# Modulation loads on GpSimd's queue, the last head's output kept on chip, and the first gate multiplied into the output weights

## The chip, the cores and the metric

The kernel runs on one core of a Trainium2 chip. The core has TensorE (PE, matrix products), VectorE (DVE), ScalarE (ACT), GpSimd (POOL) and SyncE (SP, which here only starts transfers), each of which works through its own instructions in order, and 16 DMA engines. The metric is the device time of one execution in microseconds (us), the median of several runs.

## The reference

One layer of a transformer block on x of 1024 positions by 1024 features, with six vectors of modulation from a conditioning vector c. Cut to what matters:

```python
mod = silu(c) @ w_ada + b_ada
sh_m, sc_m, gt_m, sh_f, sc_f, gt_f = split(mod, 6)

h = rms_norm(x, g_mix) * (1 + sc_m) + sh_m
qa, ka, va, qb, kb, vb = split(h @ w_in)
o_a = neighbourhood_attention(qa, ka, va, rpb)         # 8 heads of 64
o_b = differential_attention(qb, kb, vb, lam, slopes)  # 4 heads, two maps each
o_b = rms_norm(o_b, subln_w) * (1 - lambda_init)       # per head
mix = concat(o_a, o_b) @ w_out
x = x + gt_m * mix

h = rms_norm(x, g_ffn) * (1 + sc_f) + sh_f
gate, up = split(h @ w_gate_up)
x = x + gt_f * ((silu(gate) * up) @ w_down)
out = rms_norm(x, g_final)
```

All is float32. The gate gt_m scales columns of mix, so it may as well scale the columns of w_out.

## The kernel before

Each product of two float32 matrices is made of three passes on PE: both factors are split into a high part and a rest (names ending in h and l), and high by high, rest by high and high by rest are summed in PSUM. For every operand ACT makes the high part and DVE or POOL subtracts it (line 202 for weights, a raw tile of 128x1024 with the suffix r from one of two buffers). Matrix products are mostly 128x512.

The stages follow each other. **Start-up**: x is loaded, normalised (`rs` on POOL, a scaling on DVE) and turned; the first two modulation vectors are summed up on DVE. **Attention**: 64 units in a row, `Na` for four pairs of neighbourhood heads of eight units each, then `Da` for four differential heads of eight units. A unit has a score, a softmax on DVE and ACT, a turn of the weights on PE (`nt` or `at`) and a product with v (`npv` or `pv`). The loop over units calls the score of the next unit, `pv` of the last, norm and finish of those before, and between these `fill`, which takes products of the input projection (`q`, `k`, `v`) for later heads out of a queue. When these are done (last unit of the third `Da` head), `load_late` reads back the first four blocks of the attention's output from DRAM (`ol`), splits them and loads half of the output weights (`wo`); then `gen_mo` makes the first half of the output projection (blocks n = 0 to 3, tiles `mo`) as filler of the last head, multiplies each tile by the gate (`mt`) and adds it to x.

**The drain**: the last unit's `pv`, its norm (`ms`, `rda`, `bc`), and its store to DRAM. Then pool `mx` closes, `lp` takes its memory, and blocks 4 to 7 are loaded and split into it with the other half of the weights. The second half of the projection (tiles `mp`, n = 4 to 7) runs, each tile is multiplied by the gate (`mu`, line 1053) and added (line 1054, on POOL up to i = 5). **norm2** and the **feed-forward** stage (`gu` gate and up, `dn` down) follow.

**Modulation**: vectors 2 to 5 are summed by `gen_mods` (lines 570 to 607), a generator taken one step per unit: each half vector has eight steps, a load `wm` of 256 KB and a multiply-add into `acc` on DVE. Vectors 2, 3 and 4 (48 loads) run during attention; 2 is `gate_m`. Vector 5, `gate_f`, runs beside the first feed-forward group. All these loads are issued by SP. The bias tables of a pair, `tz`, are loaded by SP in `tables` when the pair starts.

The order in the program: in the start-up and for the first two units, PE, DVE, ACT and SP keep the order in which the code is written, while POOL does not; behind that a scheduler places instructions on every engine by their dependences and by its own estimate of when they are ready. Pools with a number of buffers (bufs) make a writer wait until the reader of the buffer's last tile is done.

Of the kernel before, what the change touches and what calls it, by code (L numbers as in the profile page):

```python
# [19 lines left out]
P = 128  # L20
# [84 lines left out]
def block_kernel(ctx: ExitStack, tc: tile.TileContext, t: dict):  # L105
# [449 lines left out]

    def tables(pr):
        tb = []
        for m in range(2):
            h = 2 * pr + m
            tbh = np_.tile([P, 896], F32, tag="tb", bufs=2, name=f"tb{h}")  # L560
            tz = mp.tile([P, 384], F32, tag="sq", bufs=4, name=f"tz{h}")
            z = t["rpb"]
            SY.dma_start(out=tz, in_=bass.AP(tensor=z.tensor, offset=z.offset + 512 * h + 1, ap=[[1, P], [1, 384]]))
# [7 lines left out]
    def gen_mods(steps, raw_of, acc_of, tmp_of, gate, ahead=2):  # L571
# [76 lines left out]
    class Da:  # L648
# [90 lines left out]
        def finish(self):  # L739
# [114 lines left out]
    def gate_m():  # L854
        if 2 not in gates:
# [4 lines left out]
                    lambda nm, dt=F32: mp.tile([P, 512], dt, tag="sq", bufs=4, name=nm), gate_m)  # L860
# [3 lines left out]
    def load_o(n, pool, **kw):  # L864

        if n % 4 == 0:
            for z, lst in (("h", oh), ("l", ol)):
                lst.append([pool.tile([P, 4, 512], F32R, name=f"o{z}{n}{b}", **kw) for b in range(2)])
        for b in range(2):
            SY.dma_start(out=ol[n // 4][b][:, n % 4, :].bitcast(F32), in_=o_dram[n][:, b * 512:(b + 1) * 512])  # L870

    def split_o(n):
        for b in range(2):
            dh, dl = oh[n // 4][b][:, n % 4, :], ol[n // 4][b][:, n % 4, :]
            A.activation(out=dh, in_=dl.bitcast(F32), func=AF.Copy)
            V.tensor_tensor(out=dl, in0=dl.bitcast(F32), in1=dh.bitcast(F32), op=ALU.subtract)

    def load_wo(dh, n2, split):
        raw = raw_t(f"wo{dh}_{n2}r")
        SY.dma_start(out=raw, in_=t["w_out"][dh, n2])  # L880
        wo[dh].append(split(raw, f"wo{dh}_{n2}"))

    def load_late():
        lo_eng[:] = [V]
        for n in range(4):
# [302 lines left out]
```

## Time and profile before

| what | us |
|---|---|
| median of three runs | 1437.06 (1435.95 to 1438.21) |
| the profiled execution | 1438.62 |
| its span, first to last instruction | 1436.9 |
| PE busy | 1375.6 |
| DVE, ACT, POOL busy | 736.2, 462.7, 275.6 |

The mean granted clock of PE was 0.974 of full speed. Busy time counts no waits, no DMA issues and no semaphores; PE's matrix products overlap, so a full-speed product of 128x512 shows some 390 ns of its own though the next begins about 227 ns after it. A row of a timeline names the instruction by its line, its engine and its tiles (out<-in), and in brackets the idle time before it and what ended that. All products have line 89, a helper's. The window from 8 to 60 us is the start-up, attention lasts until about 641 us, the drain until about 708 and the feed-forward stage to the end.

### The profile page before, as it was taken

How to read it: one execution, taken by the hardware profiler on the slowest of the kernel's cores; microseconds unless marked ns; L12 is line 12 of the kernel's file. 1: busy time of each engine (PE TensorE's matmuls, PEld its weight loads, DVE VectorE, ACT ScalarE, POOL GpSimd, SP SyncE). 2: the span in 40 equal slices, each digit the busy share in tenths (PEclk: the TensorE clock that was granted, in tenths of full speed). 3: DMA queues.
4: the chain of work that ended last, by engine and by line, in shares of the span. 5: the costliest groups of instructions: out<-in, count | busy, mean ns of one | idle time of the engine just before them, and what ended most of it. 6: DMA issues, size and time to landing. Idle time of an engine off the chain costs nothing.

```text
span 1436.9 us, 17706 instructions
## 1 busy us (share of the span) xinstructions
PE 1375.6 (96%) x7033; PEld 1137.9 (79%) x7033; DVE 736.2 (51%) x1336; ACT 462.7 (32%) x817; POOL 275.6 (19%) x274
## 2 busy tenths in 40 slices
PE   5899998899999999988999999999999999999997
PEld 5698777787897777766878888888888888888886
DVE  5775866758777587767737315212411431152136
ACT  5544444444544464423440210211021111202212
POOL 3021221210002100003430420422132122204201
PEclk8999998999999999998999999999999999999999
DMA  9231522423021251006111210211021111102102
GB/s 380 91 118 48 182 99 83 151 95 111 23 89 59 96 198 38 8 29 221 59 44 59 88 31 29 82 36 59 15 73 59 30 59 59 44 16 88 44 15 103
DMA packets 47826, 115.34 MB, mean 80 GB/s; under 512 B 12755, under 2 KB 14035, under 8 KB 46464
## 3 DMA queue, kind: packets, MB, share of 16 engines
q1 hardware_dynamic: 47632, 114.05, 23.4%
q8 instruction: 55, 0.90, 0.3%
q14 instruction: 27, 0.22, 0.0%
q0 software_dynamic: 112, 0.17, 0.0%
HBM read 99.52 MB, written 14.68 MB: 79 GB/s over the span
## 4 chain that ended last, share of the span: by engine, by line
PE 86%; DMA 6%; DVE 5%; issue 1%; ACT 1%; SPq 0%; POOL 0%; DVEq 0%; POOLq 0%; ACTq 0%
PE gu L89 33%; PE dn L89 17%; PE s L89 4%; PE mo L89 3%; PE q L89 3%; PE pv L89 3%; PE k L89 3%; PE mp L89 2%; PE nk L89 2%; DMA wm<-in_w_ada_l_dram 2%; PE at L89 2%; PE v1p L89 2%; PE npv L89 2%; PE v2p L89 2%; DMA w_r<-in_w_in_dram 2%; PE sps L89 2%
## 5 line engine op out<-in xcount | busy, mean ns | idle before, releaser
L1095 DVE TENSOR_TENSOR sg<-sg,gu 128x512 f32<-128x512 f32 x44 | 30.2, 687 | 354.5 <-ACT sg L1094 354.3
L89 PE MATMUL dn<-wd_l,ah 128*128 128x512 f32 x352 | 137.0, 389 | 0.0
L89 PE MATMUL dn<-wd_h,al 128*128 128x512 f32 x352 | 137.0, 389 | 0.0
L89 PE MATMUL dn<-wd_h,ah 128*128 128x512 f32 x352 | 137.0, 389 | 0.0
L1125 DVE TENSOR_TENSOR dt<-dn,gate_f 128x512 f32<-128x512 f32 x96 | 66.3, 691 | 87.7 <-PE dn L89 87.7
L202 POOL TENSOR_TENSOR wg_l<-wg_r,wg_h 128x1024 fp32r<-128x1024 f32 x20 | 47.9, 2396 | 295.6 <-ACT wg_h L201 295.6
L201 ACT ACTIVATE wg_h<-wg_r 128x1024 fp32r<-128x1024 f32 x22 | 23.3, 1061 | 225.3 <-PE dn L89 165.7
L675 ACT ACTIVATE p<-p,st 128x1024 f32<-128x1024 f32 x64 | 73.4, 1148 | 68.3 <-DVE st L673 68.0
L673 DVE CUSTOM_DVE_ANT_0 p<-s,dist 128x1024 f32<-128x1024 f32 x64 | 76.6, 1218 | 16.2 <-PE s L89 16.0
L89 PE MATMUL s<-qk 64*128 64x512 f32 x384 | 80.4, 427 | 2.2 <-DVE st L673 2.1
L202 POOL TENSOR_TENSOR wd_l<-wd_r,wd_h 128x1024 fp32r<-128x1024 f32 x20 | 47.9, 2397 | 161.1 <-ACT wd_h L201 161.1
L89 PEld LDWEIGHTS dn<-wd_l,ah 128*128 128x128 f32 x352 | 66.1, 188 | 13.7
L89 PEld LDWEIGHTS dn<-wd_h,al 128*128 128x128 f32 x352 | 66.1, 188 | 13.7
L89 PEld LDWEIGHTS dn<-wd_h,ah 128*128 128x128 f32 x352 | 66.1, 188 | 13.7
L1126 DVE TENSOR_TENSOR x<-x,dt 128x512 f32<-128x512 f32 x96 | 70.0, 729 | 2.9
L89 PE MATMUL gu<-h2h,wg_h 128*128 128x512 f32 x176 | 68.6, 390 | 1.9 <-DVE sg L1095 1.9
L202 POOL TENSOR_TENSOR w_l<-w_r,w_h 128x1024 fp32r<-128x1024 f32 x19 | 47.3, 2497 | 119.7 <-ACT w_h L201 113.1
L1094 ACT ACTIVATE sg<-gu 128x512 f32<-128x512 f32 x44 | 25.9, 589 | 137.1 <-PE gu L89 133.3
L89 PE MATMUL gu<-h2l,wg_h 128*128 128x512 f32 x176 | 68.5, 389 | 0.0
L89 PE MATMUL gu<-h2h,wg_l 128*128 128x512 f32 x176 | 68.5, 389 | 0.0
L89 PE MATMUL gu<-h2l,wu_h 128*128 128x512 f32 x176 | 68.5, 389 | 0.0
L89 PE MATMUL gu<-h2h,wu_l 128*128 128x512 f32 x176 | 68.5, 389 | 0.0
(287 smaller groups left out, 3483.7 us busy)
## 6 DMA issues: line engine op xcount, KB each, us to landing
wm<-in_w_ada_l_dram SPq DMA_DIRECT2D x64, 256.0 KB, 3.7
w_r<-in_w_in_dram SPq DMA_DIRECT2D x24, 512.0 KB, 4.2
wg_r<-in_w_gate_up_dram SPq DMA_DIRECT2D x22, 512.0 KB, 3.6
wu_r<-in_w_gate_up_dram SPq DMA_DIRECT2D x22, 512.0 KB, 3.5
wd_r<-in_w_down_dram SPq DMA_DIRECT2D x22, 512.0 KB, 3.5
x<-in_x_dram SPq DMA_DIRECT2D x16, 512.0 KB, 8.8
wada<-in_w_ada_s_dram SPq DMA_DIRECT2D x6, 1024.0 KB, 12.1
v<-vd SPq DMA_DIRECT2D x4, 1024.0 KB, 4.9
```

Of the source, the lines that this page charges most:

```text
L89: ins = call(*args, **kw)
L201: A.activation(out=hi, in_=raw, func=AF.Copy)
L202: lo_engine().tensor_tensor(out=lo, in0=raw, in1=hi.bitcast(F32), op=ALU.subtract)
L673: V.tensor_tensor_reduce(out=pr, in0=s, in1=dists[0][:, d0:d0 + 1024], scale=1.0, scalar=BIG, op0=ALU.add, op1=ALU.min, accum_out=self.st[ ...
L675: A.activation(out=pr, in_=pr, func=AF.Exp, scale=-1.0, bias=self.st[:, m:m + 1], accum_out=self.st[:, 2 + m:3 + m])
L1094: A.activation(out=sg, in_=gu[:, 0:512], func=AF.Silu)
L1095: V.tensor_tensor(out=sg, in0=sg, in1=gu[:, 512:1024], op=ALU.mult)
L1125: V.tensor_tensor(out=dt_, in0=out, in1=gtf[:, dsl], op=ALU.mult)
L1126: V.tensor_tensor(out=x1[i][:, dsl], in0=x1[i][:, dsl], in1=dt_, op=ALU.add)
```

## The change

It has three parts. The loads `wm` of vectors 2 to 4 are issued by GpSimd instead of SyncE, and so are the table loads `tz`, which are now started at the seventh unit of the pair before (for the first pair at the beginning); vector 5's loads stay with SyncE, and its first accumulation is placed behind the last add of the output projection. The first gate is multiplied into the raw output weights before they are split, eight multiplies of 128x1024 on DVE, and `mt` and `mu` are gone: tiles are added to x straight from PSUM, by DVE alone. And the last half head's output goes into a raw buffer (`o_last`) and is split from there, with no store and no reload; blocks 4 and 5 and the weights `wo0_2` and `wo1_2` are loaded at the last unit but one into a buffer of the attention's pool, four products' worth of tiles (`mpb0`, `mpb1`) are begun before the norm, and only blocks 6 and 7 and `wo0_3`, `wo1_3` are loaded behind it.

```diff
+    def load_tables(pr):
+        for m in range(2):
+            h = 2 * pr + m
+            tzs[h] = mp.tile([P, 384], F32, tag="sq", bufs=4, name=f"tz{h}")
+            z = t["rpb"]
+            G.dma_start(out=tzs[h], in_=bass.AP(tensor=z.tensor, offset=z.offset + 512 * h + 1, ap=[[1, P], [1, 384]]))
...
-    def gen_mods(steps, raw_of, acc_of, tmp_of, gate, ahead=2):
+    def gen_mods(steps, raw_of, acc_of, tmp_of, gate, queue, first=None, ahead=2):
...
-                SY.dma_start(out=raws[-1], in_=t["w_ada_l"][which - 2, n, :, j, :])
+                queue.dma_start(out=raws[-1], in_=t["w_ada_l"][which - 2, n, :, j, :])
...
-                V.tensor_scalar(out=acc, in0=raws[at], scalar1=silc[:, 0:1], scalar2=None, op0=ALU.mult)
+                head = V.tensor_scalar(out=acc, in0=raws[at], scalar1=silc[:, 0:1], scalar2=None, op0=ALU.mult)
+                if first is not None:
+                    PE.after(head, first)
...
+            if h == 3 and half:
+                late_t["o"] = raw_t("o_last")
+                V.tensor_tensor(out=late_t["o"][:, 0:512], in0=self.us, in1=bc, op=ALU.mult)
+                return
...
+    def split_o(n, last=None):
         for b in range(2):
+            dh, dl = o_at[n, b]
+            full = last if b and last is not None else dl.bitcast(F32)
+            A.activation(out=dh, in_=full, func=AF.Copy)
+            V.tensor_tensor(out=dl, in0=full, in1=dh.bitcast(F32), op=ALU.subtract)
...
         SY.dma_start(out=raw, in_=t["w_out"][dh, n2])
+        both = raw.rearrange("p (a n) -> p a n", a=2)
+        gate = late_t["gtm"][:, dh * 512:(dh + 1) * 512].unsqueeze(1).to_broadcast([P, 2, 512])
+        V.tensor_tensor(out=both, in0=both, in1=gate, op=ALU.mult)
         wo[dh].append(split(raw, f"wo{dh}_{n2}"))
...
-            V.tensor_tensor(out=tt, in0=out, in1=late_t["gtm"][:, dsl], op=ALU.mult)
-            V.tensor_tensor(out=x1[i][:, dsl], in0=x1[i][:, dsl], in1=tt, op=ALU.add)
+            yield from mo_part(out, dh, i, range(4))
+            V.tensor_tensor(out=x1[i][:, dsl], in0=out, in1=x1[i][:, dsl], op=ALU.add)
...
+        if nx is seq[-1]:
+            spare = qp_.tile([P, 4, S], F32R, tag="qk", name="spare")
+            for m in (4, 5):
+                for b in range(2):
+                    o_at[m, b] = tuple(spare[:, 2 * m - 8 + z, b * 512:(b + 1) * 512] for z in range(2))
+                load_o(m)
+            for dh in range(2):
+                load_wo(dh, 2, lambda raw, nm: split_w(raw, gp, nm))
+                split_o(4 + dh)
...
-    fill(5)
+    while queue:
+        fill(9)
+    outs = [big(f"mpb{i}") for i in range(2)]
+    for i in range(2):
+        for dh in range(2):
+            run(mo_part(outs[i][:, dh * 512:(dh + 1) * 512], dh, i, (4, 5)))
     seq[-1].norm(units)
-    fill(5)
     seq[-1].finish()
...
-    for n in range(4):
-        if n % 2 == 0:
-            load_wo(0, 2 + n // 2, split_l)
-        load_o(4 + n, lp, tag="o", bufs=4)
-        split_o(4 + n)
-    for n2 in (2, 3):
-        load_wo(1, n2, split_l)
+    for n in (6, 7):
+        here = lp.tile([P, 4, 512], F32R, tag="o", bufs=4, name=f"o{n}")
+        for b in range(2):
+            o_at[n, b] = here[:, b, :], here[:, 2 + b, :]
+        load_o(n, (0, 1) if n == 6 else (0,))
+    for dh in range(2):
+        load_wo(dh, 3, split_l)
+        split_o(6 + dh, late_t["o"][:, 0:512] if dh else None)
...
-            V.tensor_tensor(out=tt, in0=out, in1=gtm[:, dsl], op=ALU.mult)
-            (G if i < 6 else V).tensor_tensor(out=x1[i][:, dsl], in0=x1[i][:, dsl], in1=tt, op=ALU.add)
+            done = V.tensor_tensor(out=x1[i][:, dsl], in0=out, in1=x1[i][:, dsl], op=ALU.add)
```

The scheduler's order changes with it. On PE, before, behind the last head's norm (`bc`) at once come tiles of the second half, which need blocks 4 to 7:

```order
L89 MATMUL bc_1_6154<-ident,rda_1_6144 128x128 x4
L89 MATMUL mp_0_6228<-wo_2_h,oh_6177 128x512
L89 MATMUL mp_0_6228<-wo_2_h,ol_6179 128x512
L89 MATMUL mp_0_6228<-wo_2_l,oh_6177 128x512
...
L89 MATMUL mp_0_6228<-wo_3_h,oh_6177 128x512
```

Now there stand products of blocks 4 and 5 (`spare`) for tiles of i = 2 and 3, and then the first with block 6 (`o_6194`):

```order
L89 MATMUL bc_1_6179<-ident,rda_1_6169 128x128 x4
L89 MATMUL mp_2_6258<-wo_2_h,spare 128x512 x2
L89 MATMUL mp_2_6258<-wo_2_l,spare 128x512
...
L89 MATMUL mp_3_6302<-wo_2_l,spare 128x512
L89 MATMUL mpb_6138<-wo_3_h,o_6194 128x512 x2
```

Between them the six products of four tiles, 24 in all, have moved behind `bc`. On SP, before, at that place the last head's store (`o_dram_118`), eight loads and the weights of blocks 4 to 7:

```order
L749 DMA o_dram_118<-o_0_6000 128x512
L749 DMA o_dram_118<-o_1_6159 128x512
L870 DMA ol_6179<-o_dram_115 128x512
L870 DMA ol_6180<-o_dram_115 128x512
...
L870 DMA ol_6180<-o_dram_118 128x512
L880 DMA wo_2r<-in_w_out_dram 128x1024
L880 DMA wo_3r<-in_w_out_dram 128x1024
```

And now, where `o_6194` and `o_6197` are blocks 6 and 7 and `wm_6863` is the first load of vector 5:

```order
L893 DMA wo_2r<-in_w_out_dram 128x1024
L762 DMA o_dram_117<-o_1_5645 128x512
L882 DMA spare<-o_dram_115 128x512 x2
L882 DMA spare<-o_dram_116 128x512 x2
L762 DMA o_dram_118<-o_0_6009 128x512
L893 DMA wo_3r<-in_w_out_dram 128x1024
L882 DMA o_6194<-o_dram_117 128x512 x2
L882 DMA o_6197<-o_dram_118 128x512
L587 DMA wm_6863<-in_w_ada_l_dram 128x512
L893 DMA wo_3r<-in_w_out_dram 128x1024
```

The second store of `o_dram_118` is gone, the loads of blocks 4 and 5 stand ahead of the first, and three loads of outputs are left behind. On POOL the loads come in between other work; the difference at the start-up (`rs_305` belongs to the last block of x, `pth` is a buffer of the first attention units):

```order
 L185 TENSOR_TENSOR rs_298<-rs_298,mhalf 128x1
+L587 DMA wm_713<-in_w_ada_l_dram 128x512
+L587 DMA wm_715<-in_w_ada_l_dram 128x512
 L184 TENSOR_SCALAR rs_305<-ssq_303 128x1
+L587 DMA wm_717<-in_w_ada_l_dram 128x512
 L185 TENSOR_TENSOR rs_305<-rs_305,mhalf 128x1
 L438 DMA lamv<-in_lambdas_dram 128x256
...
+L563 DMA tz_648<-in_rpb_dram 128x384
+L563 DMA tz_650<-in_rpb_dram 128x384
+L587 DMA wm_797<-in_w_ada_l_dram 128x512
```

Three loads now stand in front of the last `rs`, and the tables and the next load follow it.

## Rows read from the trace of the kernel before

**Rows 1.** The page, busy time of each engine: us, share of the span, instructions.

```profile
PE 1375.6 (96%) x7033; PEld 1137.9 (79%) x7033; DVE 736.2 (51%) x1336; ACT 462.7 (32%) x817; POOL 275.6 (19%) x274
```

**Rows 2.** What PE waited for, whole span: us in total, times, longest.

```profile
PE mp L89 <- ACT oh L875: 6.1, 1, 6.1
PE mp L89 <- DVE mu L1053: 2.2, 1, 2.2
PE bc L89 <- DVE rda L736: 1.9, 1, 1.9
PE gu L89 <- DVE sg L1095: 1.9, 1, 1.9
PE mp L89 <- ACT wo_h L201: 0.9, 1, 0.9
```

**Rows 3.** Timeline of SyncE in the drain: start us, us, instruction, count.

```profile
643.24 3.85 SPq L870 DMA_DIRECT2D ol<-o_dram  x8
647.92 0.33 SPq L880 DMA_DIRECT2D wo_3r<-in_w_out_dram  x1
```

**Rows 4.** Timeline of ScalarE in the drain; in brackets idle time before, and releaser.

```profile
647.37 2.44 ACT L875 ACTIVATE oh<-ol 128x512 fp32r<-128x512 f32 x4 [7.91 <-DMA ol<-o_dram]
```

**Rows 5.** Windows at half clock: us, PE busy (instructions), granted clock, DMA share, GB/s.

```profile
641.98:652.22 10.24, 4.19 (x9) 0.50 0.77 259
669.28:672.70 3.42, 3.42 (x9) 0.50 0.78 268
218.73:228.97 10.24, 6.82 (x19) 0.50 0.54 155
```

**Rows 6.** Timeline of PE behind the drain's hole, two products in a row.

```profile
656.11 0.39 PE L89 MATMUL mp<-wo_h,oh 128*128 128x512 f32 x1
656.34 0.39 PE L89 MATMUL mp<-wo_h,ol 128*128 128x512 f32 x1
```

**Rows 7.** The DMA list: issues, queue, count, KB each, median us to landing.

```profile
wm<-in_w_ada_l_dram SPq DMA_DIRECT2D x64, 256.0 KB, 3.7
x<-in_x_dram SPq DMA_DIRECT2D x16, 512.0 KB, 8.8
lamv<-in_lambdas_dram POOLq DMA_DIRECT2D x1, 128.0 KB, 6.9
wo_3r<-in_w_out_dram SPq DMA_DIRECT2D x2, 512.0 KB, 5.8
```

**Rows 8.** Groups of DVE, 504 to 720: busy us, mean ns, idle before.

```profile
L926 DVE TENSOR_TENSOR mt<-mo,gate_m 128x512 f32<-128x512 f32 x16 | 11.0, 688 | 10.6 <-PE mo L89 10.5
L1053 DVE TENSOR_TENSOR mu<-mp,gate_m 128x512 f32<-128x512 f32 x16 | 10.9, 686 | 7.2 <-PE mp L89 3.6 <-POOL x L1054 1.7 <-POOL r L185 1.3
L1040 DVE TENSOR_SCALAR n2v<-n2t,AB 128x512 f32<-128x512 f32 x9 | 7.1, 805 | 5.9 <-ACT h2h L1039 5.9
L202 DVE TENSOR_TENSOR ext<-wo_1r,ext 128x1024 fp32r<-128x1024 f32 x1 | 1.2, 1217 | 0.0
```

**Rows 9.** Window: us, PE, PEld, DVE, ACT, POOL busy, PEclk, DMA, GB/s.

```profile
504.00:552.00 48.00, 43.34 (x243) 33.90 (x243) 42.69 (x81) 29.91 (x51) 1.01 (x1) 0.91 0.47 176
```

**Rows 10.** The chain of waits, 139 to 345 us: a table load.

```profile
143.36 3.57 DMA tz<-in_rpb_dram
```

**Rows 11.** Timeline of PE: the holes behind table load and bursts.

```profile
158.81 0.84 PE L89 MATMUL nt<-ident,np 128*128 128x128 f32 x6 [1.67 <-DVE ptl L801]
217.01 0.44 PE L89 MATMUL nt<-ident,np 128*128 128x128 f32 x2 [2.84 <-DVE np L790]
221.57 1.54 PE L89 MATMUL nt<-ident,np 128*128 128x128 f32 x6 [3.03 <-DVE nst L771]
```

**Rows 12.** Timeline of POOL in the start-up, a DMA issue.

```profile
26.68 0.95 POOL L438 DMA_DIRECT2D lamv<-in_lambdas_dram  x1
```

**Rows 13.** Timeline of DVE between the second and third pair.

```profile
206.86 2.77 DVE L591 SCALAR_TENSOR_TENSOR acc<-wm,silc,acc 128x512 f32<-128x512 f32 x1
212.66 0.75 DVE L591 SCALAR_TENSOR_TENSOR acc<-wm,silc,acc 128x512 f32<-128x512 f32 x1 [0.98 <-DMA wm<-in_w_ada_l_dram]
```

More of the change, by code (lines that the diff above doesn't have):

```diff
@@ L559, in tables @@
             h = 2 * pr + m
+            tz = tzs[h]
             tbh = np_.tile([P, 896], F32, tag="tb", bufs=2, name=f"tb{h}")
-            tz = mp.tile([P, 384], F32, tag="sq", bufs=4, name=f"tz{h}")
-            z = t["rpb"]
-            SY.dma_start(out=tz, in_=bass.AP(tensor=z.tensor, offset=z.offset + 512 * h + 1, ap=[[1, P], [1, 384]]))
             for d0, s0, n in ((0, 0, 384), (384, 128, 256), (640, 0, 256)):
@@ L884, in load_late @@
         lo_eng[:] = [V]
+        late_t["gtm"] = gates[2]
+        for b in range(2):
+            hi, lo = (gp.tile([P, 4, 512], F32R, tag="t8", bufs=8, name=f"o{z}{b}") for z in "hl")
+            for n in range(4):
+                o_at[n, b] = hi[:, n, :], lo[:, n, :]
         for n in range(4):
-            load_o(n, gp, tag="t8", bufs=8)
+            load_o(n)
         for n in range(4):
@@ L901, in load_late, with mo_part @@
             load_wo(1, n2, split(n2))
[L903 removed]
+    def mo_part(out, dh, i, ns):
         isl = slice((i % 4) * P, (i % 4 + 1) * P)
[L906 removed]
+        for n in ns:
             w_h, w_l = wo[dh][n // 2]
             wsl = slice((n % 2) * 512, (n % 2 + 1) * 512)
[L909 removed]
+            a_h, a_l = (z[:, isl] for z in o_at[n, i // 4])
             for ti, (a, w) in enumerate([(a_h, w_h), (a_l, w_h), (a_h, w_l)]):
@@ L912, in mo_part, with run @@
             yield 0.65
+    def run(gen):
+        for _ in gen:
+            pass
     def gen_mo(dh):
@@ L984, in block_kernel @@
     wl = ctx.enter_context(tc.tile_pool(name="wl", bufs=8, reuse_waits="tile"))
-    spare = qp_.tile([P, 4, S], F32R, tag="qk", name="spare")
     pairs = [0]
@@ L994, in split_l @@
         return split_w(raw, wl, name, tag="w")
-    late_t["tmp"] = (lp, "sil", 3)
-    gtm = late_t["gtm"]
-    for n in range(4):
-        if n % 2 == 0:
-            load_wo(0, 2 + n // 2, split_l)
-        load_o(4 + n, lp, tag="o", bufs=4)
-        split_o(4 + n)
-    for n2 in (2, 3):
-        load_wo(1, n2, split_l)
+    for n in (6, 7):
+        here = lp.tile([P, 4, 512], F32R, tag="o", bufs=4, name=f"o{n}")
+        for b in range(2):
+            o_at[n, b] = here[:, b, :], here[:, 2 + b, :]
[3 more added lines that the diff above has]
+        split_o(6 + dh, late_t["o"][:, 0:512] if dh else None)
     PE.hold = PE.last
-    while queue:
-        fill(9)
     ssq2 = sm.tile([P, NT], F32, tag="ssq2", bufs=1, name="ssq2")
@@ L1047, in block_kernel @@
         for dh in range(2):
-            out = bank(f"mp{dh}_{i}")
-            for _ in mo_part(out, dh, i, 1):
-                pass
+            if i < 2:
+                out = outs[i][:, dh * 512:(dh + 1) * 512]
+                run(mo_part(out, dh, i, (6, 7)))
+            else:
+                out = bank(f"mp{dh}_{i}")
+                run(mo_part(out, dh, i, range(4, 8)))
             dsl = slice(dh * 512, (dh + 1) * 512)
-            tt = lp.tile([P, 512], F32, tag="sil", bufs=3, name=f"mu{dh}_{i}")
-            V.tensor_tensor(out=tt, in0=out, in1=gtm[:, dsl], op=ALU.mult)
-            (G if i < 6 else V).tensor_tensor(out=x1[i][:, dsl], in0=x1[i][:, dsl], in1=tt, op=ALU.add)
+            done = V.tensor_tensor(out=x1[i][:, dsl], in0=out, in1=x1[i][:, dsl], op=ALU.add)
             if 2 * i + dh > 10:
@@ L1101, in block_kernel @@
                               lambda nm: lp.tile([P, 512], F32, tag="macc", bufs=1, name=nm),
-                              lambda nm, dt=F32: lp.tile([P, 512], dt, tag="sil", bufs=3, name=nm), lambda: gtf):
+                              lambda nm, dt=F32: lp.tile([P, 512], dt, tag="sil", bufs=3, name=nm), lambda: gtf, SY, late_t["done"]):
                 pass
```

42 lines of the change are left out of this document (15 added, 27 removed).

## The prediction

> **What bounds the kernel now.** I read the busy line first: TensorE (PE) works 1375.6 of 1436.9 us, 96% [rows 1]. So the kernel is bound by its multiplications, which this change leaves alone, and the most that any edit of waits can give is the 61 us in which PE is idle, and what a lowered clock adds to the work beside those holes. The list of what PE waited for says which holes these are [rows 2]. The largest that is no load of the start-up is the first product of the second half of the output projection, which waits 6.1 us for `oh`; near it stand 0.9 us for `wo_h` and 2.2 us for `mu`. These three lie within 30 us, in the drain behind the last attention head. Others lie between pairs of heads, and 1.9 us at the first gate-up tile (`gu`).
>
> Next I followed the drain engine by engine. SyncE issues eight `ol` loads from 643.24 us on, in 3.85 us, and only then the weights `wo_3` at 647.92 [rows 3]; ScalarE starts the first split at 647.37, after 7.91 us without work [rows 4]. So the wait is a round trip through DRAM: write the last head's output, read everything back, split it. The windows at half clock price the echo [rows 5]: 1.2 GHz from 641.98 to 652.22 us with 4.19 us of PE work, and again from 669.28 to 672.70 with 3.42 us. At 2.4 GHz that work takes half, so 2.1 + 1.7 = 3.8 us are lost. The drain's price is 6.05 + 0.9 + 2.2 + 3.8 = **13.0 us**, without the head's own norm chain.
>
> **Part 1: the last output stays on chip, and more is loaded before it.** What goes: one store, one reload, and the place of `o4`, `o5`, `wo_2` behind the norm; their loads and splits now come before the last unit's end. In the order, PE goes from `bc` straight into 24 products of `mp0_2` to `mp1_3`. At the full-speed step, 656.34 - 656.11 = 0.23 us [rows 6], they last 24 x 0.227 = 5.4 us and run over the loads of `o6`. Those have no new start: they still wait for PE to be done with the memory, so they issue at about 643.2, land 4.1 us later as `ol` did (643.24 to 647.37 [rows 3, 4]) and are split by 648.0, against PE done, from the end of `bc` at 642.0 [rows 6], at 647.4: 0.6 us uncovered. `wo0_3` comes from DVE: `o_last`, one split, its gate multiply and then ScalarE's split (four halves in 2.44 us [rows 4], so 1.2 for two), 0.7 + 0.7 + 1.2 + 1.2 us from 642.1 is 645.9, hidden; its low half queues on DVE behind `o6`'s and is due near 649.9, and PE reaches it after eight products, at 649.8. `wo1_3` needs a raw slot that `o_last` occupies until about 644: landing 5.8 us as `wo_3r` did [rows 7], then 2.4 us for gate and split, gives 652, just before PE wants it (24 products behind 648.0, 653.4). So about 1 us returns here, 0 at best, 4 at worst if the loads of the modulation and of the feed-forward weights slow these down. The norm chain's 1.9 us before `bc` [rows 6] stay, since `bc` still comes last behind `rda`, and I keep one half-clock stretch of 3.4 us behind it, 1.7 us. Net: -13.0 + 1.7 + 1.0 = **-10.3 us**, between -13 and -6.
>
> The 2.2 us wait for `mu` goes for another reason: `mu` stood on DVE behind accumulations of the last modulation, which waited for their loads. They are now pinned behind the last add of the projection. There DVE idles 5.9 us before `n2v` [rows 8], and eight steps of 0.75 us are 6 us of work; but if loads make them longer, `n2v`, `sg` and PE's 1.9 us wait at `gu` [rows 2] follow: 0 to +4 us, I take 0.
>
> **Part 2: the gate in the weights.** DVE loses 16 multiplies of `mt` and 16 of `mu` at 0.69 us (22 us) [rows 8]; it gains eight weight multiplies, nearest row the 1.22 us split of the same two-input shape (9.8 us), and takes 12 adds over from GpSimd (some 8 us at the same 0.69). That is -4 us on DVE, none of it on PE's path as such. Its one dangerous place is where the first four heads' outputs are split: from 504 to 552 us DVE is busy 42.69 of 48 us and PE idles 4.7 us at a clock of 0.91 [rows 9]. Three gate multiplies fall there, 3.7 us of DVE, while few `mt` leave. If each pushed PE, +4 us; if the moved loads loosen it, -3. I take 0, since two of the eight are placed well ahead and PE has products to fill with.
>
> **Part 3: 48 modulation loads and 8 table loads on GpSimd's queue.** SyncE is freed: a modulation load that waits for DVE's accumulate no longer holds up what is queued behind it. A table load `tz` stands in the chain of waits at 143 us with 3.57 us [rows 10] and now runs a pair ahead; but PE's hole next behind it is 1.67 us [rows 11], so that is all that can return there, and the accumulate steps are next late. I count -1.
>
> Against it: the order puts GpSimd's loads between its memsets, its weight splits and, in the start-up, ahead of `rs7`. A load's issue takes GpSimd 0.95 us [rows 12] against SyncE's 0.33 (`wo_3r` [rows 3]). In the start-up, up to three of them stand before `rs7`, which PE's first products need: 0 to 2.85 us, I take 1. Later the price per load that DVE waits for lies between the issue's 0.6 us and 3.2 us, the difference of 6.9 us (`lamv`, the only long one on this queue) and 3.7 (`wm`) [rows 7]. `lamv` ran in the crowded start-up, and `x` loads of SyncE's own took 8.8 us there [rows 7], so I go near the low end. One burst waits for two loads (DVE is held 2.77 us at 206.86 and 0.98 us at 212.66 [rows 13]), and four bursts matter: 8 x 0.6 = 5 us of DVE time, of which PE, with filler between, should see about 2. Ends: -1 (nothing was late) and +20 (all eight at 3.2, less cover). Net of part 3 with start-up: -1 + 1 + 2 = **+2 us**.
>
> The Trainium skill speaks against this part: "DMA: Bandwidth & Descriptors", section "Issuing engine by pattern", sends simple loads to Sync, and the page's opening table gives about 1 us to the first byte from GpSimd's queue against 0.6; by that alone eight waited loads cost an estimated 3 us. "SBUF — State Buffer" adds, in its box on the "DVE blocks DMA" trap, that GpSimd cannot write descriptors while VectorE runs a two-port operation. No row here shows either apart, the queue carries three loads only; the sum does without both.
>
> **The sum.** Added up, against the profiled execution's 1438.62 us (span 1436.9 and 1.7 around it): 1438.6 - 10.3 + 0 + 2 = 1430.3. The median shown is 1.56 us lower, so on its scale 1428.7; I say **1428.5**.
>
> **Rivals.**
> *GpSimd's queue becomes the bound (slower).* Place: the accumulate bursts at each pair's start. GpSimd works in order; a load behind a weight split, and a memset behind a load that waits for an accumulate, lengthen each burst, and the first score of the next pair stands behind the burst on DVE. At 3.2 us for each of eight waited loads less a third hidden, 17 us, and two more half-clock stretches of 1.7: 1428.5 - 2 + 20 = 1447. It decides against the change from +10 us of such waits on, 1.3 us a load. For it: those holes exist already (`nt` 3.03 [rows 11], clock 0.50 from 218.73 us [rows 5]). Against: GpSimd is busy 19%, and most bursts have filler over them.
> The box of the Trainium skill named above leads to this rival too; its price here is worked out from rows alone, and no run shows its mechanism yet.
>
> *The drain's wait only moves.* The 24 products cover `o6` but `wo_3`, both raw slots and the splits on DVE come late, or `gu` inherits the pinned accumulations: half of the 10 us is lost, 1434 to 1440, no difference worth the name.
>
> *The transitions gain too.* SyncE's queue no longer stands behind DVE; if that was why the pairs start late, the holes of 2.84 and 3.03 us before 217 and 221.6 us [rows 11] and 3.4 us of clock (6.82 us of work at half clock [rows 5]) go as well: up to 9 us, 1419 to 1422.
>
> **How the numbers follow.** Forecast (1422 to 1434): 0.57. Transitions gain: 0.14. Drain moves: 0.14. GpSimd's queue bounds: 0.15. What a measurement can tell here is 0.2%, 2.9 us: faster means under 1434.2, slower over 1439.9. Faster 0.57 + 0.14 = 0.71, within 0.14, slower 0.15. The range 1418 to 1441 leaves out the far half of both outer cases, under 0.2.
>
> **What would show it.** Right: PE's wait for `oh` is gone from its list, `mu`'s too; the hole behind `bc` is under 2 us, and from 642 to 653 us PE is busy over 8 us where it had 4; the feed-forward stage, which has no hole of PE behind `gu`'s, keeps its length. Wrong in part 3: `wm` takes over 5 us to land, PE's waits at `npv` and `nt` grow by over 5 us, or a wait for a memset of `pth` appears. Wrong in part 2: idle between 504 and 552 us over 6 us. Wrong in part 1: a wait of `mpb` or `mp` for `wo_h` or `ol` over 2 us, or of `gu` for `sg` over 4. The prediction as a whole falls if the gain in the drain is below 6 us or the first 504 us grow by over 5.

## The result, and the profile after

The changed kernel took 1427.4 us, median of four runs (1423.15 to 1428.33), the kernel before 1436.51: a ratio of 0.9937, 95% interval 0.9921 to 0.9953. Run again on another occasion it was 1425.88 us, ratio 0.9928 (0.9903 to 0.9953). So it is faster by 9 to 10 us, 0.6 to 0.7%; the two intervals together allow 7 to 14 us. The forecast was 1428.5 with a range of 1418 to 1441. The number held; not all of its terms did, and the experiments below show which. One execution of a later variant (`u_gate` below) took 4756 us; it is left out of that kernel's time.

The profiled execution of the first set was its fastest (1423.15 us). I read its drain, and take the lengths of stages from the profile of the second set (called `again` below), whose 1428.04 us are nearer to the median. It is the slowest of its four executions, and the profile of the kernel before, at 1438.62 us, lies above its median too.

First the busy line of the changed kernel's page, as in [rows 1], and four lines of the list of what PE waited for, as in [rows 2] (us in total, times, longest); the others belong to the start-up or come to 2.9 us or less each:

```profile
PE 1378.5 (97%) x7033; PEld 1142.2 (80%) x7033; DVE 724.2 (51%) x1324; ACT 461.9 (32%) x817; POOL 291.5 (21%) x318
```

```profile
PE nt L89 <- DVE nst L784: 3.9, 1, 3.9
PE ns L89 <- DVE nst L784: 2.3, 1, 2.3
PE bc L89 <- DVE rda L745: 1.6, 1, 1.6
PE gu L89 <- DVE sg L1126: 0.4, 1, 0.4
```

No wait of `mp` for `oh`, `mu` or `wo_h` is left in that list. The drain's timeline of PE (start, us, instruction, count, idle before), first the norm's product `bc` of the kernel before, whose hole and end the prediction used and which is not among [rows 6], then the changed kernel:

```profile
641.35 0.65 PE L89 MATMUL bc<-ident,rda 128*128 128x128 f32 x4 [1.91 <-DVE rda L736]
```

```profile
644.90 0.79 PE L89 MATMUL bc<-ident,rda 128*128 128x128 f32 x4 [1.60 <-DVE rda L745]
645.34 1.20 PE L89 MATMUL mp<-wo_h,spare 128*128 128x512 f32 x2
...
652.46 1.07 PE L89 MATMUL mpb<-wo_h,o 128*128 128x512 f32 x4
```

The hole before `bc` is there, 1.60 us, and behind it PE goes on without one: products of blocks 4 and 5 (`spare`), then from 652.46 us of block 6. SyncE and ScalarE, beside [rows 3, 4]:

```profile
614.87 1.75 SPq L882 DMA_DIRECT2D spare<-o_dram  x4
...
634.20 0.80 SPq L882 DMA_DIRECT2D o<-o_dram  x2
```

```profile
646.52 0.63 ACT L888 ACTIVATE o<-o_last 128x512 fp32r<-128x512 f32 x1 [5.08 <-DVE o_last L758]
647.05 0.61 ACT L888 ACTIVATE o<-o 128x512 fp32r<-128x512 f32 x1
```

Blocks 4 and 5 were fetched at 614.87 and block 6 at 634.20, ten microseconds before `bc`; ScalarE splits block 6 at 647.05, five microseconds before PE wants it. The clock in the drain and in the stretch of [rows 9] (us, PE busy, granted clock, DMA share, GB/s):

```profile
645.27:648.68 3.41, 3.41 (x11) 0.50 0.02 5
529.22:542.87 13.65, 13.30 (x43) 0.50 0.52 197
504.00:552.00 48.00, 47.51 (x244) 0.86 0.48 176
```

One half-clock stretch of 3.41 us in the drain, where [rows 5] had 10.24 and 3.42. From 504 to 552 us idle fell from 4.66 to 0.49 us, but the clock there is 0.86 where it was 0.91: 13.65 us in one piece at 1.2 GHz.

Now the stages, cut at the first neighbourhood score, the first differential score, the first product of the output projection, its last, and the first down product. Columns: us, PE busy, granted clock, DMA share, GB/s; first the kernel before, then the changed one (`again`).

```profile
86.46:325.53 239.07, 225.01 (x1475) 0.96 0.33 105
325.53:551.70 226.17, 219.84 (x1307) 0.97 0.27 97
551.70:707.04 155.34, 144.03 (x723) 0.94 0.18 63
```

```profile
87.06:318.71 231.65, 222.74 (x1463) 0.98 0.34 106
318.71:555.89 237.18, 234.45 (x1323) 0.94 0.27 95
555.89:696.48 140.59, 138.99 (x723) 0.99 0.15 50
```

Neighbourhood heads -7.4 us, differential heads **+11.0 us**, last head and drain **-14.7 us**; the start-up, norm2 and the feed-forward stage make +0.6. The sum is -10.6, the span's difference (1436.9 to 1426.3).

The 11 us in the differential heads are the one thing that the prediction did not see coming (6.6 us in the first profile, where that stage took 232.80 us). Idle fell there (6.3 to 2.7 us), yet the stage is longer. Two rows show the larger cause. The page's group of the score products `s` (count, busy us, mean ns, idle before), before and after:

```profile
L89 PE MATMUL s<-qk 64*128 64x512 f32 x384 | 80.4, 427 | 2.2 <-DVE st L673 2.1
```

```profile
L89 PE MATMUL s<-qk 64*128 64x512 f32 x384 | 88.6, 425 | 2.9 <-DVE st L682 2.9
```

The same 384 products keep PE busy 8.2 us longer. Each product has 64 rows, half of the array; a unit has two maps, on rows 0 to 63 and 64 to 127. Where products of the two maps stand next to each other they start together. In the timeline of the kernel before, a unit of twelve takes 1.65 us; in the changed kernel six of one map alone take as long:

```profile
405.30 1.65 PE L89 MATMUL s<-qk 64*128 64x512 f32 x12
```

```profile
526.05 1.64 PE L89 MATMUL s<-qk 64*128 64x512 f32 x6
```

Counted over the trace (two starts within 0.05 us), there are 98 such pairs before and 63 after; 35 fewer at one step of 0.227 us would be 7.9 us. That step is too high. Take from PE's busy time half of what it did at 1.2 GHz (the "lost" time below), and its work at full speed is left: 1375.6 - 27.1 = 1348.5 us over the whole span before, 1378.5 - 24.1 = 1354.4 in the first profile and 1384.7 - 31.2 = 1353.5 in `again`. So the change added 5 to 6 us of work; if all of it is the pairs', that is 0.15 to 0.17 us for each, and the experiments with more pairs below give 0.18. That the scheduler pulls the two maps apart because the second map's PSUM buffer becomes free later is only argued. The rest in this stage is clock: 7.0 us are lost there before and 15.3 in `again` (10.1 in the first profile). Together, in `again`, the stage has 6.3 us more work (six products `q` among it that stood a stage earlier), 8.3 more lost clock and 3.6 less idle time, which makes the 11.0.

### The profile page after: what moved, and what is told of

It reads as the page before. It is cut to its first block, busy times and chain, and to the rows that moved or that the text cites. A ratio compares the mean times of both kernels' runs of the same rounds, so it can differ in the third digit from the quotient of the medians.

```text
span 1421.4 us, 17696 instructions
## 1 busy us (share of the span) xinstructions
PE 1378.5 (97%) x7033; PEld 1142.2 (80%) x7033; DVE 724.2 (51%) x1324; ACT 461.9 (32%) x817; POOL 291.5 (21%) x318
## 4 chain that ended last, share of the span: by engine, by line
PE 90%; DVE 4%; ACT 2%; DMA 1%; issue 1%; POOL 1%; POOLq 0%; DVEq 0%; ACTq 0%
PE gu L89 33%; PE dn L89 17%; PE s L89 5%; PE pv L89 3%; PE mo L89 3%; PE k L89 3%; PE q L89 3%; PE mp L89 3%; PE at L89 2%; PE nk L89 2%; PE npv L89 2%; PE v1p L89 2%; PE v2p L89 2%; PE nq L89 1%; PE v3p L89 1%
## 5 line engine op out<-in xcount | busy, mean ns | idle before, releaser
L89 PE MATMUL s<-qk 64*128 64x512 f32 x384 | 88.6, 425 | 2.9 <-DVE st L682 2.9
L89 PEld LDWEIGHTS dn<-wd_h,al 128*128 128x128 f32 x352 | 66.1, 188 | 13.7
L89 PEld LDWEIGHTS dn<-wd_l,ah 128*128 128x128 f32 x352 | 66.1, 188 | 13.7
L89 PEld LDWEIGHTS s<-qk 64*128 64x128 f32 x384 | 54.3, 189 | 26.0 <-issue 9.0
L89 PE MATMUL gu<-h2h,wu_h 128*128 128x512 f32 x176 | 68.6, 390 | 0.0
```

Of the source, the lines that this page charges most:

```text
L89: ins = call(*args, **kw)
```

## The experiments

Ratios are to the kernel before, on the same chip (1436.3, 1434.5 and 1436.6 us in the three groups); differences in us are to the changed kernel's 1426. Where "idle" and "lost" are given for a stage, idle is its length less PE's busy time, and lost is half of PE's busy time in the stretches at half clock.

**The changed kernel again.**

> The changed kernel once more, on the chip of the other runs of this group, as what they are compared with. All theories: 1427 us, ratio to before 0.994; the profile after (1423.2 us) was the lowest of four times, and this one should show where the 4 us between it and the others (1427.3 to 1428.3) go: by the granted clock of 0.974 against 0.979 in one or two more half-clock stretches of about 3.4 us in attention, not in the drain.

1425.88 us. Its profile is 4.9 us longer than the first: 7.1 us more are lost to the clock, and idle and work are 2.2 shorter. Of the lost time 5.2 us lie in the differential heads, where the longest of the differing stretches ran from 322.09 to 332.33 us here (331.25 to 334.66 there), and 2.0 in the start-up. So the difference between these two executions of one kernel is such stretches.

**Part 3, the queue.** Undone for the loads alone (`u_sync`):

```diff
-                    lambda nm, dt=F32: mp.tile([P, 512], dt, tag="sq", bufs=4, name=nm), gate_m, G)
+                    lambda nm, dt=F32: mp.tile([P, 512], dt, tag="sq", bufs=4, name=nm), gate_m, SY)
...
-            G.dma_start(out=tzs[h], in_=bass.AP(tensor=z.tensor, offset=z.offset + 512 * h + 1, ap=[[1, P], [1, 384]]))
+            SY.dma_start(out=tzs[h], in_=bass.AP(tensor=z.tensor, offset=z.offset + 512 * h + 1, ap=[[1, P], [1, 384]]))
```

> The changed kernel with the modulation and table loads back on SyncE's queue (tables still a pair ahead). Prediction's sum: GpSimd's queue costs 2 us net, so 1425. Rival (SyncE's queue behind VectorE's accumulates held up the pair transitions, and freeing it is the gain between 86 and 318 us, where idle TensorE fell from 14.1 to 9.2 us): 1432 or more, with idle back over 13 us there. A third reason would act in either direction: the scheduler's order holds 79 adjacent pairs of score products of the two maps, against 64 in the changed kernel and 104 in the kernel before; at 0.227 us a pair that alone is -3.4 us.

1425.43 us, ratio 0.9928 (0.9903 to 0.9954): no difference. The rival that SyncE's freed queue makes the gain falls: idle between 85 and 317 us is 8.6 us here, 8.9 in `again`. In the start-up GpSimd's queue does cost: idle is 17.2 us here against 19.0, and over all profiles of kernels with the change it is 17.2 to 18.3 us with SyncE's queue (four) and 18.3 to 21.0 with GpSimd's (eight). The DMA list of the changed kernel shows that the queue is no slower for the same load (beside [rows 7]):

```profile
wm<-in_w_ada_l_dram POOLq DMA_DIRECT2D x48, 256.0 KB, 3.5
lamv<-in_lambdas_dram POOLq DMA_DIRECT2D x1, 128.0 KB, 8.5
```

3.5 us to landing (3.7 in `again`) where SyncE's took 3.7; an issue took GpSimd 0.54 us in the median. `lamv`, with 8.5, is the start-up's crowding and not its queue: there the first three `wm` took 7.2 to 8.5 us on GpSimd's queue here and 9.7 to 11.1 on SyncE's in the kernel before.

Undone wholly, with the tables loaded when their pair starts (`u_tables`):

```diff
-        if u.pos < 3 and u.i == 6:
-            load_tables(u.pos + 1)
...
     def tables(pr):
+        load_tables(pr)
```

> The changed kernel with part 3 wholly undone: modulation and table loads on SyncE's queue, and the tables loaded when a pair starts. u_sync kept the tables a pair ahead and had 8.6 us of idle TensorE between 85 and 317 us, where the kernel before has 14.1. If the early tables are what lowered it: idle of 12 to 14 us there, 1428 to 1430. Rival (the gain there comes from the order that the scheduler finds, which any edit shifts): idle of 8 to 10 us, 1425.

1424.14 us, ratio 0.9909 (0.9888 to 0.9930), with the first theory's idle and the rival's time. Idle between 86 and 324 us is back at 13.3 us, so it was the early tables that lowered it. But the kernel takes no more time for it. The window rows of the two (both on SyncE's queue), tables early and then late:

```profile
84.90:317.11 232.21, 223.64 (x1465) 0.97 0.34 106
317.11:553.78 236.67, 231.06 (x1317) 0.94 0.27 94
```

```profile
85.78:323.94 238.16, 224.83 (x1474) 0.96 0.33 105
323.94:552.98 229.04, 225.87 (x1308) 0.96 0.28 96
```

The early tables win 6.0 us in the neighbourhood heads and lose 7.6 in the differential ones, where the clock falls from 0.96 to 0.94 and idle grows by 2.4. That is one profile each, and lost clock alone differs by 5 us in that stage between two of one kernel, so why the next stage gives the gain back is not shown; the timed runs agree that none is left. Part 3 as a whole is worth nothing that can be measured.

**Part 1, the output on chip.** First the store and the reload put back, blocks 4 and 5 still early (`u_store`):

```diff
-            if h == 3 and half:
-                late_t["o"] = raw_t("o_last")
-                V.tensor_tensor(out=late_t["o"][:, 0:512], in0=self.us, in1=bc, op=ALU.mult)
-                return
...
-        load_o(n, (0, 1) if n == 6 else (0,))
+        load_o(n)
...
-        split_o(6 + dh, late_t["o"][:, 0:512] if dh else None)
+        split_o(6 + dh)
```

> The changed kernel with the last half head's output stored and read back, as block 7's second half; blocks 4 and 5 still early. If the early blocks and their 24 products are what fills the hole behind the norm: 1427 to 1428, because the round trip (store about 2 us, load about 4, split 0.6: 649.5 counted as in the kernel before) ends before its first product, 16 products behind 648. Rival (keeping the output on chip is what removes the wait): a wait of 2 to 4 us returns behind the norm with its half-clock stretch, 1430 to 1433.

1430.27 us, ratio 0.9956 (0.9942 to 0.9970), 4.4 us over the changed kernel by the medians, though the intervals overlap. The time is the rival's, without its wait: no hole comes back behind the norm, and the one before `bc` is 1.60 us, as it was. From the first product of the output projection to the first down product it is 1.5 us longer than `again` (`gu` waits 1.1 us for `sg` instead of 0.3); 2.4 us more lie in the differential heads, 1.2 of them lost clock and 1.1 idle, in one profile each. That keeping the last output removes the hole is refuted; in the drain it is worth some 1.5 us.

Then the early loads put back too, by moving the code that loads and splits blocks 4 and 5 behind the norm and dropping `mpb` (`u_part1`):

```diff
-        if nx is seq[-1]:
-            spare = qp_.tile([P, 4, S], F32R, tag="qk", name="spare")
...
+    spare = qp_.tile([P, 4, S], F32R, tag="qk", name="spare")
+    for m in (4, 5):
+        for b in range(2):
+            o_at[m, b] = tuple(spare[:, 2 * m - 8 + z, b * 512:(b + 1) * 512] for z in range(2))
+        load_o(m)
```

> The changed kernel with part 1 undone: the last output is stored and read back, and blocks 4 and 5 with their weights, like 6 and 7, are loaded and split only behind the norm; gate in the weights and GpSimd's queue stay. The score products stand in the same 64 pairs as in the changed kernel. Prediction's sum for part 1: 10.3 us, so 1426 + 10 = 1436, with a wait of mp for o of 5 to 7 us behind the norm and half clock over 8 us there; the same kernel with the store alone put back was 1430, so early blocks are worth some 6. Rival (the gain is made before the drain, by the early tables and the order): 1430 or less.

1429.65 us, ratio 0.9952 (0.9931 to 0.9973). That looked as if part 1 were worth 3 to 4 us. But SyncE's timeline shows that the early loads were not undone:

```profile
622.55 1.94 SPq L878 DMA_DIRECT2D spare<-o_dram  x4
...
648.41 1.92 SPq L878 DMA_DIRECT2D o<-o_dram  x4
```

Blocks 4 and 5 go into `spare`, a buffer that is free early, and the scheduler moved their loads up to 622.55 us by itself. Where the data go decides here, not where the code stands. So the blocks were given the home that they had in the kernel before, memory of the pool that opens when the attention's closes (`u_home`). (The edit also puts the loads and weights back into the order of the kernel before, the weights `wo_2` with them, and lets another tile of norm2 use `spare`; this is its heart:)

```diff
-            o_at[m, b] = tuple(spare[:, 2 * m - 8 + z, b * 512:(b + 1) * 512] for z in range(2))
+    for n in (4, 5, 6, 7):
+        here = lp.tile([P, 4, 512], F32R, tag="o", bufs=4, name=f"o{n}")
+        for b in range(2):
+            o_at[n, b] = here[:, b, :], here[:, 2 + b, :]
```

> The changed kernel with blocks 4 to 7 and their weights loaded behind the norm into the memory that the attention's pool gives back, as the kernel before does; gate in the weights, GpSimd's queue and the pin stay. In u_part1 the blocks 4 and 5 lay in a buffer that is free early, and their loads were issued at 622.6 us in spite of their place in the code, so it did not undo the early loads. Prediction's price of part 1: the hole of 6 us for o and half clock over 10 us there return, but not mu's 2.2 us: 1426 + 6.5 + 2 = 1434 to 1436. Rival (the gate in the weights is what empties the drain): 1428 to 1430.

1443.07 us, ratio 1.0042 (1.0026 to 1.0059): 17 us over the changed kernel and 13 over the last one, from which only this edit separates it. That is more than expected, and slower than the kernel before. Two of its waits, SyncE's timeline, and its windows, cut as above, of the differential heads and of last head and drain:

```profile
PE mp L89 <- ACT o L884: 6.2, 1, 6.2
PE mp L89 <- ACT wo_h L201: 2.2, 1, 2.2
```

```profile
651.38 4.81 SPq L878 DMA_DIRECT2D o<-o_dram  x8
...
656.77 0.37 SPq L889 DMA_DIRECT2D wo_3r<-in_w_out_dram  x1
```

```profile
320.26:559.59 239.33, 235.74 (x1322) 0.93 0.27 94
559.59:713.39 153.80, 143.82 (x723) 0.96 0.15 50
```

The eight loads stand behind the norm again, and the hole of 6 us with them; PE now waits 2.2 us for `wo_h` where it was 0.9, and ScalarE, before it can split `wo_2`, 1.95 us for VectorE's gate multiply. The drain's idle is 10.0 us against 1.6, its lost clock 4.2 against 1.6, and last head and drain together are 13.2 us longer. So the mechanism of part 1 is shown, and it is the home of blocks 4 and 5. That the kernel is slower than the one before does not come from last head and drain (153.8 us against 155.3) but from the differential heads, 239.3 us against 226.2, with fewer pairs (66) and 16.4 us of lost clock against 7.0.

**Part 2, the gate in the weights.** The tiles multiplied again, in the changed kernel (`u_gate`):

```diff
-            done = V.tensor_tensor(out=x1[i][:, dsl], in0=out, in1=x1[i][:, dsl], op=ALU.add)
+            tt = lp.tile([P, 512], F32, tag="sil", bufs=3, name=f"mu{dh}_{i}")
+            V.tensor_tensor(out=tt, in0=out, in1=late_t["gtm"][:, dsl], op=ALU.mult)
+            done = (G if i < 6 else V).tensor_tensor(out=x1[i][:, dsl], in0=x1[i][:, dsl], in1=tt, op=ALU.add)
```

(and the same for `mt`, with both operations on VectorE; the gate multiply in `load_wo` left out.)

> The changed kernel with the gate multiplied into each tile again (mt and mu on VectorE, the adds of mu on GpSimd up to tile 5), the rest as changed. Prediction: 0 for the gate, so 1426. The order holds 77 adjacent score pairs against 64, which by 0.227 us each is -3: 1423. Rival (the gate multiplies take VectorE's time between 504 and 552 us, or relieve it behind the norm): idle of TensorE there 2 us lower or 2 to 5 us of waits of mp for mu behind the norm, 1428 to 1431.

1442.97 us, ratio 1.0053 (1.0033 to 1.0074): 17 us over the changed kernel, where the prediction had 0 for this part; the rival had the waits right, not their price. Three of its waits, GpSimd's adds, and the same two windows:

```profile
PE mp L89 <- DVE mu L1084: 3.7, 1, 3.7
PE mpb L89 <- DVE mu L1084: 1.4, 1, 1.4
PE gu L89 <- DVE sg L1127: 1.4, 1, 1.4
```

```profile
668.42 2.20 POOL L1085 TENSOR_TENSOR x<-x,mu 128x512 f32<-128x512 f32 x1 [12.89 <-DVE mu L1084]
673.86 2.52 POOL L1085 TENSOR_TENSOR x<-x,mu 128x512 f32<-128x512 f32 x2 [3.24 <-DVE mu L1084]
```

```profile
319.03:560.73 241.70, 237.77 (x1323) 0.91 0.27 93
560.73:710.23 149.50, 142.47 (x720) 0.98 0.14 45
```

With blocks 4 and 5 done early, eight half-finished tiles (four of `mpb`, four of `mp`) come to their end close together. Each must pass `mu` into one of three buffers and then an add on GpSimd of 1.3 us (2.20 beside a weight split on VectorE); PE's next tile waits for the bank, 3.65 us at 676 us. In the kernel before, tiles ended one by one, and the same pair of operations kept up but for the one wait of 2.2 us. (VectorE also makes norm2's scalings and weight splits between these `mu`; whether the buffers, the adds or this other work holds PE up most, no run separates.) Idle in the drain is 5.4 us more than in `again`, at `gu` 1.1, clock there 1.8; that and 1.8 us of work make 10 of the 15 us between the two profiles. The rest is the differential heads, 4.5 us longer: clock from 530.31 to 554.21 us, 23.9 us at 1.2 GHz instead of 13.7, 6.9 us lost more in that stage, 1.2 more idle and 3.6 less work, with 78 pairs. Why the clock fell for longer there is not shown. As in the last experiment, last head and drain are shorter than in the kernel before (149.5 us against 155.3); what makes this kernel slower than that one is the differential heads, 241.7 us against 226.2.

The pin alone taken out (`u_pin`):

```diff
-                              lambda nm, dt=F32: lp.tile([P, 512], dt, tag="sil", bufs=3, name=nm), lambda: gtf, SY, late_t["done"]):
+                              lambda nm, dt=F32: lp.tile([P, 512], dt, tag="sil", bufs=3, name=nm), lambda: gtf, SY):
```

> The changed kernel without the pin that holds the last modulation's accumulations behind the projection's last add. Prediction: VectorE then waits for their loads among the adds of the tiles, a wait of mp of about 2.2 us with 1.7 us of half clock returns, 1429 to 1430. Rival (with the multiplies of mu gone the adds have slack enough, four PSUM banks cover it): 1426, and gu's wait for sg below 0.4 us.

1425.83 us, ratio 0.9940 (0.9920 to 0.9960): the rival. With `mu` gone, accumulations between the adds delay nobody; a wait of 0.2 us is all. None of them waits for its load here, so whether the missing multiply or loads that are in time is what saves the adds, this run does not separate.

**The pairs.** The score products tied in turn, second map first, as its buffer is the later one (`pair_a`):

```diff
+    tied = [None]
+
-    def scores(dsts, q, k, qsl, ksl):
+    def scores(dsts, q, k, qsl, ksl, tie=False):
...
-            for m in range(2):
+            for m in ((1, 0) if tie else (0, 1)):
...
-                PE.matmul(dsts[m], q[z][r, qsl], k[w][r, ksl], start=ti == 0, stop=ti == 2)
+                mm = PE.matmul(dsts[m], q[z][r, qsl], k[w][r, ksl], start=ti == 0, stop=ti == 2)
+                if tie:
+                    if tied[0] is not None:
+                        PE.after(mm, tied[0])
+                    tied[0] = mm
```

> The changed kernel with the score products of the two maps of a differential head tied into one order, map 1 and map 0 in turn, so that two products of 64 rows stand next to each other: 181 adjacent pairs in the program's order instead of 64. Theory (two neighbours run at once, as 98 pairs in the trace before and 63 after do, and each lone product costs TensorE 0.227 us that nothing hides): 1427.4 - 117 x 0.227 = 1401 us. Rival (the scheduler had them apart because the second map's buffer comes free later, so that TensorE waits for VectorE instead): 1422 to 1430, with waits of s for st in place of the gain.

1406.15 us, ratio 0.9797 (0.9774 to 0.9819), 20 us faster than the changed kernel. The group of scores in its page:

```profile
L89 PE MATMUL s<-qk 64*128 64x512 f32 x384 | 69.3, 446 | 7.5 <-DVE st L688 7.5
```

174 pairs in the trace, 69.3 us busy instead of 88.6 (91.1 in `again`), and 7.5 us of waits for VectorE instead of 2.9, so the rival takes 4.6 us. PE's work at full speed is 20.5 us shorter than in the first profile, for 111 pairs: 0.18 us each and not 0.227. With 5.1 us more idle and 3.2 less lost clock, 18.7 us are left between the two profiles; 26 were expected.

> The kernel before with only the score products of the two maps tied in turn: 179 adjacent pairs instead of 104. If pairs are worth 0.227 us each: 1436.3 - 75 x 0.227 = 1419, less up to 3 us of new waits as pair_a showed (it got 20 of 27 us): 1419 to 1424; the drain's waits (oh 6.1, mu 2.2) stay as they are. Rival (the gain of pair_a depends on the change): 1433 or more. The difference of pair_a (1406) to this one is then the change without its cost in pairs: 13 to 18 us by the first.

1428.92 us, ratio 0.9957 (0.9941 to 0.9974): 5.5 us, less than half of what was expected. In its profile, which like that of the changed kernel's first set was the lowest time, PE's work at full speed is 14.4 us shorter (78 pairs more, 0.18 us each) and idle 2.7 longer. That the runs show less than the profile is in part the clock: at a mean granted clock of 0.976 this kernel took 1424.45 us and the kernel before 1432.95 to 1434.47, but three of five executions ran at 0.971 to 0.973, where eight of nine of the kernel before ran at 0.974 to 0.976. Why it is lower more often stays open, and so does the rest of the difference.

Which part of the change costs the pairs stays open as well: no part that was undone above brings them back (63 to 78 in the seven kernels, 98 before).

The tied products with SyncE's queue (the edits of `pair_a` and `u_sync` together):

> Score products of the two maps tied in turn, in the changed kernel, with modulation and table loads on SyncE's queue (tables a pair ahead). u_sync had 17.2 us of idle TensorE in the start-up against 19.0 and was as fast as the changed kernel: if queue and pairs add up, 1404 to 1406. Rival (GpSimd's queue helps once the units are shorter): 1409 or more.

1403.29 us, ratio 0.9777 (0.9751 to 0.9803): the lowest median here, 2.2% below the kernel before and 1.6% below the changed one, with an interval that overlaps that of the tied products alone. With four low halves of weights moved to GpSimd besides:

```diff
     def load_late():
-        lo_eng[:] = [V]
+        lo_eng[:] = [G]
...
+        lo_eng[:] = [V]
```

> As pair_sync, with the low halves of the four weights that are split beside the third differential head (504 to 552 us) made by GpSimd instead of VectorE. VectorE is 89% busy there and GpSimd 1 us of 48. If VectorE bounds that stretch, 4.9 us less of its work: 1400 to 1403. Rival (VectorE's two-input operations wait while GpSimd works, as the accumulate of 2.77 us at 206.86 us beside a normal 0.75): no gain or a loss, 1405 to 1410.

1407.12 us, ratio 0.9795 (0.9773 to 0.9817): no gain, and by the overlapping intervals no certain loss. The rival, and its mechanism stands in two rows, of GpSimd and of VectorE:

```profile
522.97 3.08 POOL L202 TENSOR_TENSOR ext<-wo_0r,ext 128x1024 fp32r<-128x1024 f32 x1 [1.48 <-ACT ext L201]
```

```profile
523.76 3.37 DVE L902 TENSOR_TENSOR wo_1r<-wo_1r,gate_m 128x1024 f32<-128x1024 f32 x1
```

Beside GpSimd's split, VectorE's gate multiply takes 3.37 us; it takes 1.22 alone.

The kernel before had such a row too. The accumulation of 2.77 us at 206.86 us [rows 13] ran beside this weight split of GpSimd:

```profile
206.50 2.58 POOL L202 TENSOR_TENSOR w_l<-w_r,w_h 128x1024 fp32r<-128x1024 f32 x1 [6.53 <-DVE ptl L801]
```

## Why the prediction was right, point by point

**The drain, -10.3 with a range of -13 to -6.** Right in mechanism; the size is 1.7 us beyond the range: last head and drain came 14.7 us shorter, the wait of `gu` 1.6. As forecast, the norm's hole stayed (1.60 us for 1.9), and one half-clock stretch of 3.41 us behind it. One step was wrong: "those have no new start" for the loads of block 6. The memory that they wait for came free long before `bc`, and they were issued at 634.20, not 643.2. So nothing of the 1 us counted as returning did; and `wo_3` was in time as worked out. The larger difference is outside the term: of the half-clock stretches around 550 us, 2.5 us of lost time lay behind the first product of `mo` in the kernel before and none do now. Without them the gain is 12.2 us, inside the range.

**Mu's 2.2 us.** The result is right; the pin was not the reason, for without it the wait does not return (0.2 us in `u_pin`).

**Part 2, 0.** The step that failed most: it counted VectorE's work and looked at one place (504 to 552 us). Undone in the changed kernel it is worth 17 us. Some 10 us lie behind the first product of the output projection, by the timeline because part 1 lets tiles finish in a crowd, and without the gate in the weights each has two operations and a slow engine to pass; the rest is clock in the differential heads, whose cause is open. Parts 1 and 2 do not add. In last head and drain, where they act, part 1 without part 2 saves 5.8 us (155.3 to 149.5), part 2 without part 1 saves 1.5 (153.8), and both save 14.7. The prediction priced each against the kernel before, where tiles ended singly, and so had the sum right and no notion of how either half would do.

**Part 3, +2, between -1 and +20.** Measured: 0. The load's price is the low end, as chosen, and even below (3.5 and 3.7 us to landing, an issue of 0.54 us and not 0.95). One reading behind it was wrong: "DVE is held 2.77 us at 206.86" counted as a wait for a load what was an accumulation beside GpSimd's weight split. The 1 us for the start-up is 1.8 in idle. The -1 for the tables priced one hole alone; PE's idle in the neighbourhood heads fell by 5 us, and none of it is left in the time. The Trainium skill ("DMA: Bandwidth & Descriptors", section "Issuing engine by pattern") sends simple loads to Sync, which speaks for undoing this part. Here it makes no difference that can be measured. The "DVE blocks DMA" trap of the Trainium skill (the box in "SBUF — State Buffer", section "SBUF: two separate sides") did not show: the median load on this queue landed as fast as SyncE's. Whether any of VectorE's operations beside these loads was a two-port one, no run shows.

**The rivals.** GpSimd's queue as the bound did not happen. "The drain's wait only moves" did not either. "The transitions gain too" happened in the holes (idle down 5 us), not for SyncE's freed queue but for the early tables, and not in the time.

**What was not in it.** The order. The section on the change showed where loads and products moved, but I did not count what the scheduler did to products that the change never touches. The step that failed is the prediction's first, "its multiplications, which this change leaves alone": with 35 score pairs lost, PE has 5 to 6 us more work at full speed, and with the clock the differential heads are 7 to 11 us longer, where the prediction had 0. That a gain of 7 us ahead of it and 4 us more in the drain stood against it is luck: the forecast was 1 us off with errors of up to 11 us on either side.

## What to carry to other kernels

Price the parts of a change together where one alters the rhythm in which another's work arrives; the drain needed both early blocks and a one-step way out of PSUM: alone they saved 5.8 and 1.5 us there, together 14.7. A scheduled load can be as early as its buffer is free: look at the home of the data before the line of the code. And when a scheduler sets the order, compare it over products that the change does not touch; half-array products that lose their neighbour cost 0.15 to 0.18 us each here, and an explicit order for them was worth more than the whole change.

## What the runs showed of the hardware

Two products of 64 rows on the two halves of the array start together and take the time of one: twelve in 1.65 us, six alone in 1.64. The Trainium skill ("TensorEngine Tiling (Array Packing)", section "Overview") gives up to twice the speed where the contracted dimension is 64 or less. The trace agrees for neighbours, and shows the gain lost where the order puts other work or the same half next. Over whole kernels a pair more took 0.18 us from PE's work (111 pairs for 20.5 us, 78 for 14.4).

The clock fell without a hole. In the changed kernel PE's longest idle between 526 and 543 us is 0.35 us, and the clock is half from 529.22 on; ahead of it stand score products of one map alone and eight `ms` products with one column each. Between two executions of the same kernel the time lost in half-clock stretches differed by 7.1 us, and 4.9 us lay between their spans.

VectorE's operations with two inputs in SBUF are stretched beside GpSimd's weight splits: 3.37 us for 1.22, and 2.77 for 0.75 in the kernel before. Two with one input in PSUM (`atl<-at,ath` at 529.34 us, during a split from 528.30 to 530.68) took 1.28 us together, where one alone takes 0.69. So moving splits to GpSimd, busy 1 us of 48 in that place, saved VectorE less than the splits' own time, and no gain came of it.
